# Attention and output product of a hybrid decoder block: queries' low part one slot later, transfers at other slots, second half scaled in place

## The chip, the cores and the metric

The kernel runs on one core of a Trainium2 chip. A core has a matrix engine (TensorE, "PE" in the profile; its weight loads are "PEld"), a vector engine (VectorE, "DVE"), a scalar engine (ScalarE, "ACT"), GpSimd ("POOL"), and a queue engine that here only issues transfers (SyncE, "SP"). Each engine works through its own instructions in the order in which they were written, and waits at an instruction until what it needs is there. The metric is the device time of one execution in microseconds; lower is better.

## The reference, cut to what matters

One decoder layer over 2048 tokens of width 1024, in float32. Eight attention heads with a forgetting bias run beside a gated linear recurrence; both branches are normalised and gated, joined, and multiplied by `w_out`; a residual and a gated embedding follow.

```
def forgetting_attention(q, k, v, f_logit):
    c = jnp.cumsum(jax.nn.log_sigmoid(f_logit), axis=1)
    ...
    s = einsum('bhqd,bhkd->bhqk', qi, k) * scale + (ci[..., None] - c[..., None, :])
    w = softmax(where(kpos <= qpos, s, -inf))
    return einsum('bhqk,bhkd->bhqd', w, v)
...
o_attn = forgetting_attention(q, k, v, fl)
y_attn = rmsnorm(o_attn, attn_out_gain) * silu(g_attn)
o_lru  = rg_lru(causal_depthwise_conv(x_lru, conv_w, conv_b), ...)
y_lru  = rmsnorm(o_lru, lru_out_gain) * silu(g_lru)
mix = concatenate([y_attn, y_lru]) @ w_out
h = h + rmsnorm(mix, post_gain)
h = h + sigmoid(h @ w_ple_gate + b_ple_gate) * rmsnorm(p @ w_ple, ple_gain)
```

## The kernel before, in words

Every product runs three times in a reduced float32 type: an operand is split into a high part (a rounded copy, written by ACT) and a low part (the rest, original minus high part, written by DVE or POOL), and `mm3` (L61) multiplies high by high, high by low and low by high (L66, L67, L68).

The program has four stretches: projections and recurrence (to about 1060 us), attention (to about 1647 us), the output product (to about 1945 us), and the last gate product with the output. The order of all instructions is written out by hand. In the stretches touched here it hangs on **slots**: work is put down for a slot number, and the program emits slot after slot. A slot isn't a time. It fixes only the order on each engine; a transfer on SP goes out as soon as SP comes to it and its buffer is free.

**Attention.** There are 32 stages, one for each head `h` and each group `g` of 512 queries (`stages`, L1308). Stage n takes 4g+4 slots from `t0[n]`, one slot for each block of 128 keys, so a head takes 40 slots. `run_slot` (L1436) emits for a slot, in this order: what stands in `before` (transfers above all); the score pieces of the following stage (`piece`, L1220: three products into an `sbank`, of which there are three, then one DVE instruction, L1225, that adds the bias, finds the minimum `m` and frees the bank); the product with the values of three slots ago (`add_values`, L1268); the transposes of this slot's probabilities (`turn_probs`, L1256, with their split into `th` by ACT and `tl` by DVE, L52 and L58); exponentials on ACT (L1234); and last what stands in `after`. The 4g+4 score pieces of stage n are spread over the slots of stage n-1, three slots ahead, so the short stage g=0 carries two pieces in a slot.

Around that stands other work:

- `split_u` (L1162): the queries of stage n, already loaded as `qf`, are split by `scaled_split` into `qh` (ACT, L169) and `ql` (DVE, L170), both in the `after` list of slot `lo + 1`, where the stage's scores begin at slot `s0` and `lo` lies 4 or 8 slots ahead of that.
- `load_gate` (L1301, the transfer is L1303) loads a gate tile `gs`, which has two buffers; `store_y` (L1305) stores the result from the same buffer to `ya_d`. A gate load so waits for the store of two stages ago, which stands at slot `t0[n - 1] + 6`.
- `load_piece` and `split_piece` (L1110, L1119) load the next head's keys and values in eight pieces through three `kvf` buffers, six slots ahead of their split; ACT writes the high part, POOL the low part, which frees the buffer.
- Chores (L1417 to L1427) prepare `yl2_d` (the recurrence's branch, scaled) and sums of weights: loads five slots ahead, POOL's work, stores three slots behind.

**Seam.** In the last stage (from slot `last_t0`) there are no more scores, and the first three token tiles of the output product are multiplied as `fill` (L1530) in twelve slots between the attention's own products. Their sources are loaded by `load_raw` (L1503) into `yf`, and split by `x_high` and `x_low` (L1508, L1511) into one of three operand pairs `XO`.

**Output product.** `w_out` is applied with seven products in place of eight for each half `p` of the tokens (`PRODUCTS`, L1484). A token tile of 128 rows against 512 columns is two slots of twelve matrix instructions each; tile q begins at slot `2 * (q - 3)` (`begin_of`), its high part is planned three slots ahead and its low part two. Half p works on four quarters: attention rows j=0 and j=1, recurrence rows j=2 and j=3, four tiles `t` each, which lie in sixteen tiles `X` (`load_home`, L1684) and are combined in place by DVE (L1709 to L1712, executed at L1616). The attention rows must first be scaled by the normalisation of each token; these factors are spread to rows by PE (`spread_rows`, L1566) and copied by ACT (`rows_out`). Half 0 is scaled in its home tiles. Half 1's eight tiles are, in slots 5 to 23, loaded from `ya_d` into spare tiles, scaled (`scale_rows`, L1691) and stored to `ya2_d`, and loaded from there at slots 34 to 48. Within a slot the phases LOAD, COMBINE, PREP, JOB, MUL, GATE, STORE follow one another.

Of the kernel before, what the change touches and what calls it, by code (L numbers as in the profile page):

```python
# [9 lines left out]
F32 = mybir.dt.float32  # L10
F32R = mybir.dt.float32r
# [34 lines left out]
def f32(ap):  # L46
    return ap.bitcast(F32)
# [24 lines left out]
def hymba_kernel(ctx: ExitStack, tc: tile.TileContext, x, xT, pT, w_p, w_v, w_o, w_ple, w_pg,  # L72
# [19 lines left out]
    yl2_d = dram.tile([TB, P, D], F32, name="yl2_d")  # L92
    ya2_d = dram.tile([NH, P, D], F32, name="ya2_d")
    rl_d = dram.tile([1, S], F32, name="rl_d")
# [73 lines left out]
    def scaled_split(q, hi, lo):  # L168
        nc.scalar.activation(hi, q, AF.Copy, scale=QSCALE)  # L169
        nc.vector.scalar_tensor_tensor(out=lo, in0=q, scalar=QSCALE, in1=f32(hi), op0=ALU.mult, op1=ALU.subtract)  # L170
# [990 lines left out]

    def split_u(u):  # L1162
        if u.qf is not None:
# [137 lines left out]
    def load_gate(h, g, u):  # L1301
        u.gs = av.tile([P, 512], F32, name="gs")
        nc.sync.dma_start(out=u.gs, in_=gT_d[h, :, g * 512:(g + 1) * 512])  # L1303
# [15 lines left out]
    def at(d, slot, f):  # L1319
        d.setdefault(max(slot, 0), []).append(f)  # L1320
# [22 lines left out]

    def do_split(n):
        split_u(units[n])
# [90 lines left out]
    def run_slot(t, fill=None):  # L1436
# [48 lines left out]
    tiles_ = [(i, p, t) for i, p in PRODUCTS for t in range(4)]  # L1485
    X, banks, raws = [], {}, {}

# [9 lines left out]
    def source_of(q):  # L1497
        i, p, t = tiles_[q]
        if i == 2 or (i, p) == (4, 1):
            return raws[q]  # L1500
        return X[{4: 8, 1: 0, 6: 0, 7: 4, 5: 8, 3: 12}[i] + t]

# [8 lines left out]
    def x_low(q):  # L1511
        nc.vector.tensor_tensor(out=XO[q % 3][1], in0=source_of(q), in1=f32(XO[q % 3][0]), op=ALU.subtract)
# [53 lines left out]
    def spread_rows(p):  # L1566
        for t in range(0, 8, 4):
            b = G_.b[p, t] = bank3()
            for i in range(4):
                c = 8 * p + t + i  # L1570
                nc.tensor.transpose(b[:, i * P:(i + 1) * P], rstd_a[:, c:c + 1].broadcast_to([P, P]), ident)

    def rows_out(p):
        for t in range(0, 8, 4):
            nc.scalar.activation(U2_[2 * p + t // 4], G_.b.pop((p, t)), AF.Copy)

# [4 lines left out]

    MR, U2_, U3_, XT, MT = [], [], [], [], []
    turn_ = [0]
# [10 lines left out]
    def open_left():  # L1594
        pA_stack.close()
        l4 = pool_(ctx, "l4")
        MT.extend(l4.tile([P, D], F32, name=f"mt{i}") for i in range(2))
        XT.extend(l4.tile([P, D], F32, name=f"xt{i}") for i in range(3))
        XT.insert(1, X[15])
        G_.pgain = l4.tile([P, D], F32, name="pgain")  # L1600
        G_.bgate = l4.tile([P, D], F32, name="bgate")
# [16 lines left out]
    def plan_q(q):  # L1618
        i, p, t = tiles_[q]
        s = begin_of(q)  # L1620
        if i == 2 or (i, p) == (4, 1):
            if q > 3:
                plan(s - 7, LOAD, lambda: load_raw(q))
        if q > 3:
            plan(s - 3, PREP, lambda: x_high(q))
            plan(s - 2, PREP, lambda: x_low(q))
# [54 lines left out]
    def tokens_of(p, t):  # L1681
        return ya_d[:, :, (8 * p + t) * P:(8 * p + t + 1) * P].rearrange("h p t -> p h t")

    def load_home(p, j, t):  # L1684
        o = X[4 * j + t]
        if j < 2 and p == 0:
            nc.sync.dma_start(out=o.rearrange("p (h t) -> p h t", t=P), in_=tokens_of(0, 4 * j + t))
# [3 lines left out]
    def scale_rows(o, p, n):  # L1691
        o = o.rearrange("p (h t) -> p h t", t=P)
        rho = U2_[2 * p + n // 4][:, n % 4 * P:(n % 4 + 1) * P]
        tt(o, o, rho.unsqueeze(1).broadcast_to([P, NH, P]), ALU.mult)

    for n in range(8):
        o = lambda n=n: X[13 + n % 3]
        plan(5 + 2 * n, LOAD, lambda n=n, o=o: nc.sync.dma_start(out=o().rearrange("p (h t) -> p h t", t=P),
                                                                in_=tokens_of(1, n)))
        plan(8 + 2 * n, JOB, lambda n=n, o=o: scale_rows(o(), 1, n))  # L1700
        plan(9 + 2 * n, STORE, lambda n=n, o=o: nc.sync.dma_start(out=ya2_d[n], in_=o()))
    for p, times in ((0, (7, 9, 4, 24, 15, 17, 26, 29)), (1, (34, 42, 50, 58, 53, 55, 66, 68))):
        for t in range(4):
            for j in range(4):
                plan(times[j] + (t if p == 0 and j > 1 else 2 * t), LOAD, lambda p=p, j=j, t=t: load_home(p, j, t))
            if p == 0:
                for j in range(2):
                    plan((11, 13)[j] + 2 * t, JOB, lambda j=j, t=t: scale_rows(X[4 * j + t], 0, 4 * j + t))
            plan(times[4] + 2 * t, JOB, lambda t=t: tt(X[8 + t], X[4 + t], X[8 + t], ALU.add))  # L1709
            plan(times[5] + 2 * t, JOB, lambda t=t: tt(X[4 + t], X[t], X[4 + t], ALU.subtract))  # L1710
            plan(times[6] + 2 * t, JOB, lambda t=t: tt(X[t], X[8 + t], X[t], ALU.subtract))
            plan(times[7] + 2 * t, JOB, lambda t=t: tt(X[12 + t], X[12 + t], X[t], ALU.subtract))  # L1712

# [191 lines left out]
```

## Time and profile before

| | us |
|---|---|
| three timed runs | 2148.05, 2146.4, 2148.24 |
| their median | 2148.05 |
| the profiled execution's own time | 2146.39 |
| its span, first to last instruction | 2144.6 |
| PE busy | 2092.8 (98%) |
| DVE busy | 1624.0 (76%) |
| ACT busy | 1146.0 (53%) |
| POOL busy | 734.4 (34%) |
| moved by DMA | 527.31 MB, mean 246 GB/s |

A row of a group or a wait has the source line (L1225), the engine, and the tiles as out<-in. In the view of waits a row says which instruction waited for which, the total, how often, and the longest. In the view of windows a row has the stretch, its length, the busy time of each engine with its count of instructions in brackets, then the granted PE clock (1.00 is full), the share of the DMA engines that was busy, and GB/s. In the view in order of time a row has start, length, engine, line, and in square brackets the idle time of the engine just before it with what ended it. "SPq" is SP's queue.

### The profile page before, as it was taken

What the parts mean: (1) busy time and instruction counts of PE and PEld (TensorE: products, weight loads), DVE (VectorE), ACT (ScalarE), POOL (GpSimd) and SP (SyncE); (2) the same over time, 40 slices, a digit from 0 to 9 for tenths busy, and PEclk for the clock granted to TensorE, in tenths of its full rate; (3) what the DMA queues carried; (4) which work ended last, traced back from release to release, by engine and by line L of the source; (5) the groups of instructions that cost most, each with busy time, mean ns of one, the idle gap of its engine ahead of it and who ended that gap; (6) DMA issues with size and microseconds to landing.
All of it is one profiled execution on the core that took longest, in us unless ns stands there. A gap on an engine that the chain in (4) does not pass through costs nothing.

```text
span 2144.6 us, 31680 instructions
## 1 busy us (share of the span) xinstructions
PE 2092.8 (98%) x10586; PEld 1748.6 (82%) x10586; DVE 1624.0 (76%) x2693; ACT 1146.0 (53%) x1871; POOL 734.4 (34%) x633
## 2 busy tenths in 40 slices
PE   8899999999999999999999999999999999999999
PEld 6788888888988898888878788888787878888887
DVE  7677988696858877885578788887785677876665
ACT  7435755434337766663366676767674343442222
POOL 4834455332113335632035665665543000000000
PEclk9899999999999999999999999999999999999999
DMA  8498898987888889887666776777554977665553
GB/s 319 183 325 287 296 344 299 356 308 288 286 276 272 279 257 298 272 274 248 229 194 213 234 209 205 224 232 229 167 165 156 310 269 246 231 215 168 181 173 118
DMA packets 277139, 527.31 MB, mean 246 GB/s; under 512 B 27360, under 2 KB 94192, under 8 KB 276976
## 3 DMA queue, kind: packets, MB, share of 16 engines
q1 hardware_dynamic: 276832, 525.25, 73.4%
q8 instruction: 83, 1.36, 0.3%
q14 instruction: 80, 0.66, 0.1%
q10 hardware_dynamic: 144, 0.05, 0.0%
HBM read 318.75 MB, written 206.44 MB: 245 GB/s over the span
## 4 chain that ended last, share of the span: by engine, by line
PE 77%; DMA 7%; issue 5%; POOL 5%; DVE 3%; ACT 2%; SPq 1%; POOLq 0%; DVEq 0%; ACTq 0%
PE bank L67 15%; PE bank L66 15%; PE bank L68 15%; PE pbank L68 7%; PE pbank L66 7%; PE pbank L67 7%; PE sbank L66 2%; PE tbank L1261 2%; PE sbank L68 2%; PE sbank L67 2%; DMA kvf<-kT_d 1%; DMA ya_d<-gs 1%; PE obank L67 1%; PE obank L68 1%; PE obank L66 1%
## 5 line engine op out<-in xcount | busy, mean ns | idle before, releaser
L66 PE MATMUL bank<-XH,op 128*128 128x512 f32 x876 | 347.4, 397 | 0.0
L67 PE MATMUL bank<-XL,op 128*128 128x512 f32 x876 | 346.1, 395 | 0.0
L68 PE MATMUL bank<-XH,op 128*128 128x512 f32 x876 | 345.8, 395 | 0.0
L364 DVE TENSOR_TENSOR c<-bank,c 128x512 f32<-128x512 f32 x280 | 187.0, 685 | 124.2 <-PE bank L68 117.9
L58 DVE TENSOR_TENSOR tl<-tbank,th 128x512 fp32r<-128x512 f32 (+1 forms) x320 | 191.2, 607 | 72.8 <-ACT th L52 69.6
L52 ACT ACTIVATE th<-tbank 128x512 fp32r<-128x512 f32 (+1 forms) x320 | 167.5, 529 | 116.9 <-PE tbank L1261 112.3
L68 PEld LDWEIGHTS bank<-XH,op 128*128 128x128 f32 x876 | 164.7, 188 | 39.2
L66 PEld LDWEIGHTS bank<-XH,op 128*128 128x128 f32 x876 | 164.7, 188 | 39.2 <-issue 0.5
L67 PEld LDWEIGHTS bank<-XL,op 128*128 128x128 f32 x876 | 164.8, 188 | 38.9 <-issue 0.5
L1234 ACT ACTIVATE pr<-pr,m 128x640 f32<-128x640 f32 (+7 forms) x124 | 151.9, 1225 | 51.1 <-DVE m L1225 50.1
L1261 PE MATMUL tbank<-ident,pr 128*128 128x128 f32 x1088 | 172.0, 273 | 0.0
L152 POOL TENSOR_TENSOR rsm<-rs,mhalf 128x1 f32<-128x1 f32 x16 | 8.7, 541 | 445.1 <-DVE rs L151 445.1
L1261 PEld LDWEIGHTS tbank<-ident,pr 128*128 128x128 f32 x1088 | 134.2, 140 | 28.4
L66 PE MATMUL sbank<-kh,qh 128*128 128x512 f32 (+3 forms) x320 | 137.0, 428 | 20.2 <-DVE m L1225 19.3
L66 PE MATMUL obank<-th,vh 128*128 128x512 f32 (+1 forms) x320 | 123.9, 387 | 0.8 <-ACT th L52 0.8
L286 ACT ACTIVATE op<-wf 128x512 fp32r<-128x512 f32 (+1 forms) x96 | 60.0, 630 | 113.2 <-PE bank L68 85.7
L67 PE MATMUL obank<-tl,vh 128*128 128x512 f32 (+1 forms) x320 | 118.6, 371 | 1.3 <-DVE tl L58 0.2
L68 PE MATMUL obank<-th,vl 128*128 128x512 f32 (+1 forms) x320 | 117.2, 366 | 0.0
L68 PE MATMUL sbank<-kh,ql 128*128 128x512 f32 (+3 forms) x320 | 116.4, 364 | 0.0
L67 PE MATMUL sbank<-kl,qh 128*128 128x512 f32 (+3 forms) x320 | 116.3, 364 | 0.0
L67 PE MATMUL bank<-op,XH 128*128 128x258 f32 x328 | 94.9, 289 | 6.9 <-POOL op L292 4.9
L286 ACT ACTIVATE op<-ws 128x512 fp32r<-128x512 f32 (+1 forms) x72 | 45.0, 628 | 99.5 <-PE bank L68 42.2
(305 smaller groups left out, 5849.3 us busy)
## 6 DMA issues: line engine op xcount, KB each, us to landing
wo_d<-op SPq DMA_DIRECT2D x140, 512.0 KB, 4.4
op<-wo_d SPq DMA_DIRECT2D x79, 512.0 KB, 4.8
wf<-in_w_p_dram SPq DMA_DIRECT2D x80, 256.0 KB, 4.9
wh<-wo_d SPq DMA_DIRECT2D x61, 256.0 KB, 4.1
wl<-wo_d SPq DMA_DIRECT2D x61, 256.0 KB, 4.3
vo_d<-op SPq DMA_DIRECT2D x28, 516.0 KB, 3.7
wst<-wt_d SPq DMA_DIRECT2D x56, 256.0 KB, 3.5
X<-ya_d SPq DMA_DIRECT2D x24, 512.0 KB, 5.3
```

What stands on the lines that cost most here:

```text
L52: nc.scalar.activation(hi, src, AF.Copy)
L58: eng.tensor_tensor(out=lo, in0=src, in1=f32(hi), op=ALU.subtract)
L66: nc.tensor.matmul(out, lhsT=wh, rhs=xh, start=start, stop=False)
L67: nc.tensor.matmul(out, lhsT=wh, rhs=xl, start=False, stop=False)
L68: nc.tensor.matmul(out, lhsT=wl, rhs=xh, start=False, stop=stop)
L152: nc.gpsimd.tensor_tensor(out=o, in0=t, in1=mhalf[:, :n], op=ALU.pow)
L286: nc.scalar.activation(op[:, :n], self.source(i, hf), AF.Copy)
L364: nc.vector.tensor_tensor(out=o, in0=x, in1=y, op=ALU.add)
L1234: nc.scalar.activation(pr[0][:, :L], pr[0][:, :L], AF.Exp, bias=m2, scale=-1.0, accum_out=u.r4[:, i:i + 1])
L1261: nc.tensor.transpose(b[:, i * P:(i + 1) * P], u.P[i][:, sb * P:(sb + 1) * P], ident)
```

## The change

1. `split_u` takes a part: the high part stays in slot `lo + 1`, the low part goes to `lo + 2`.
2. Transfers in attention: the gate load goes from no earlier than `t0[n - 1] + 7` to no earlier than `t0[n - 1] + 10`; the loads of key and value pieces from six to four slots ahead of their split; the stores of the chores from three to five slots behind their work.
3. Seam: token tile 0 is loaded seven slots before `last_t0` into the free `bias` buffer and split at slots +1 and +2 (before: loaded at +1, split at +4 and +5). Tiles 1 to 5 are now loaded and split within the last stage (before: 1 to 3). The fill goes from slots +7 to +18 to slots +5 to +16.
4. Output product: half 1's scaling through `ya2_d` is gone. Its tiles are loaded from `ya_d` into their homes at slots 28 to 40 and scaled there at slots 35 to 48; the homes are other tiles than before (`home`), with four of them (`A1`) in the tiles of the last stretch. Half 1's factors are spread at slot 26 (before 6). The combinations of half 1 are at slots 50, 57, 66 and 74 (before 53, 55, 66 and 68).
5. With that, the weights of the last gate product move to other tiles and its first two splits to slots 66 and 70 (before 77 and 80); the load of `bgate` moves from slot 61 to slot 104.

```
-            scaled_split(u.qf, u.qh, u.ql)
+            nc.scalar.activation(u.qh, u.qf, AF.Copy, scale=QSCALE)
+        elif u.qf is not None:
+            nc.vector.scalar_tensor_tensor(out=u.ql, in0=u.qf, scalar=QSCALE, in1=f32(u.qh),
+                                           op0=ALU.mult, op1=ALU.subtract)
...
-        at(after, min(lo + 1, s0 - 1) if n > 1 else 0, lambda n=n: do_split(n))
+        at(after, lo + 1 if n > 1 else 0, lambda n=n: split_u(units[n], 0))
+        at(after, lo + 2 if n > 1 else 0, lambda n=n: split_u(units[n], 1))
...
-        at(before, max(t0[n] - 4, t0[n - 1] + 7) if n else t0[n] + 1, lambda h=h, g=g, n=n: load_gate(h, g, units[n]))
+        at(before, max(t0[n] - 4, t0[n - 1] + 10) if n else t0[n] + 1, lambda h=h, g=g, n=n: load_gate(h, g, units[n]))
...
-            at(before, a - 6, lambda h=h, p_=p_: load_piece(h, p_))
+            at(before, a - 4, lambda h=h, p_=p_: load_piece(h, p_))
...
-    at(before, a + 3, lambda h_=h_, n=n, i=i: h_(n, i))
+    at(before, a + 5, lambda h_=h_, n=n, i=i: h_(n, i))
...
+    def load_first():
+        raws[0] = pA.tile([P, D], F32, name="yf", tag="bias", bufs=1)
+        nc.sync.dma_start(out=raws[0], in_=yl2_d[0])
+
+    at(before, last_t0 - 7, load_first)
...
-    for q, a, z in ((0, 1, 4), (1, 2, 7), (2, 4, 10), (3, 6, 14)):
+    for q, a, z in ((1, 1, 4), (2, 2, 8), (3, 4, 11), (4, 6, 15), (5, 12, 19)):
...
+    at(after, last_t0 + 1, lambda: x_high(0))
+    at(after, last_t0 + 2, lambda: x_low(0))
...
-        run_slot(t, fill if last_t0 + 7 <= t < t0[NS] + AHEAD else None)
+        run_slot(t, fill if last_t0 + 5 <= t < last_t0 + 17 else None)
...
-    for p, a in ((0, 4), (1, 6)):
+    for p, a in ((0, 4), (1, 26)):
...
+    def home(p, j, t):
+        return A1[t] if (p, j) == (1, 0) else X[4 * (j - p) + t]
...
+        if j < 2:
+            nc.sync.dma_start(out=o.rearrange("p (h t) -> p h t", t=P), in_=tokens_of(p, 4 * j + t))
         else:
-            nc.sync.dma_start(out=o, in_=ya2_d[4 * j + t] if j < 2 else yl2_d[8 * p + t + 4 * (j == 2)])
+            nc.sync.dma_start(out=o, in_=yl2_d[8 * p + t + 4 * (j == 2)])
+
+    def scale_home(p, j, t):
+        o = home(p, j, t).rearrange("p (h t) -> p h t", t=P)
+        c = (XT[3] if p else X[12])[:, (4 * j + t) * P:(4 * j + t + 1) * P]
+        tt(o, o, c.unsqueeze(1).broadcast_to([P, NH, P]), ALU.mult)
...
-    for n in range(8):
-        o = lambda n=n: X[13 + n % 3]
-        plan(5 + 2 * n, LOAD, lambda n=n, o=o: nc.sync.dma_start(out=o().rearrange("p (h t) -> p h t", t=P),
-                                                                in_=tokens_of(1, n)))
-        plan(8 + 2 * n, JOB, lambda n=n, o=o: scale_rows(o(), 1, n))
-        plan(9 + 2 * n, STORE, lambda n=n, o=o: nc.sync.dma_start(out=ya2_d[n], in_=o()))
-    for p, times in ((0, (7, 9, 4, 24, 15, 17, 26, 29)), (1, (34, 42, 50, 58, 53, 55, 66, 68))):
+    for p, times in ((0, (7, 9, 4, 24, 11, 13, 15, 17, 26, 30)), (1, (28, 34, 42, 50, 35, 42, 50, 57, 66, 74))):
...
-    for k, s in enumerate((77, 80, 84, 88, 92, 96, 99, 102)):
+    for k, s in enumerate((66, 70, 83, 87, 91, 95, 99, 102)):
...
-    plan(61, LOAD, lambda: nc.sync.dma_start(out=G_.bgate, in_=rows[2:3, :].broadcast_to([P, D])))
+    plan(104, LOAD, lambda: nc.sync.dma_start(out=G_.bgate, in_=rows[2:3, :].broadcast_to([P, D])))
```

More of the change, by code (lines that the diff above doesn't have):

```diff
@@ L92, in hymba_kernel @@
     yl2_d = dram.tile([TB, P, D], F32, name="yl2_d")
-    ya2_d = dram.tile([NH, P, D], F32, name="ya2_d")
     rl_d = dram.tile([1, S], F32, name="rl_d")
@@ L1160, in load_u, with split_u @@
             u.dg.append((L - n, dg))
-    def split_u(u):
-        if u.qf is not None:
+    def split_u(u, part):
+        if u.qf is not None and part == 0:
             u.qh = ap.tile([P, 512], F32R, name="qh", bufs=2)
             u.ql = ap.tile([P, 512], F32R, name="ql", bufs=2)
-            scaled_split(u.qf, u.qh, u.ql)
+            nc.scalar.activation(u.qh, u.qf, AF.Copy, scale=QSCALE)
+        elif u.qf is not None:
+            nc.vector.scalar_tensor_tensor(out=u.ql, in0=u.qf, scalar=QSCALE, in1=f32(u.qh),
+                                           op0=ALU.mult, op1=ALU.subtract)
     def mask_u(u):
@@ L1342, in do_load @@
         load_u(*stages[n], units[n])
-    def do_split(n):
-        split_u(units[n])
     for n in range(1, NS):
@@ L1472, in run_slot @@
             f()
+    raws = {}
+    def load_first():
+        raws[0] = pA.tile([P, D], F32, name="yf", tag="bias", bufs=1)
+        nc.sync.dma_start(out=raws[0], in_=yl2_d[0])
+    at(before, last_t0 - 7, load_first)
     for t in range(last_t0 + 1):
@@ L1485, in hymba_kernel @@
     tiles_ = [(i, p, t) for i, p in PRODUCTS for t in range(4)]
-    X, banks, raws = [], {}, {}
+    X, banks = [], {}
     def bank3():
@@ L1500, in source_of @@
             return raws[q]
-        return X[{4: 8, 1: 0, 6: 0, 7: 4, 5: 8, 3: 12}[i] + t]
+        return home(p, {4: 2, 1: 0, 6: 0, 7: 1, 5: 2, 3: 3}[i], t)
     def load_raw(q):
@@ L1571, in spread_rows, with rho @@
                 nc.tensor.transpose(b[:, i * P:(i + 1) * P], rstd_a[:, c:c + 1].broadcast_to([P, P]), ident)
+    def rho(p, n):
+        return (XT[3] if p else X[12])[:, n * P:(n + 4) * P]
     def rows_out(p):
         for t in range(0, 8, 4):
-            nc.scalar.activation(U2_[2 * p + t // 4], G_.b.pop((p, t)), AF.Copy)
+            nc.scalar.activation(rho(p, t), G_.b.pop((p, t)), AF.Copy)
     G_.b = {}
@@ L1580, in hymba_kernel @@
         plan(a + 1, COMBINE, lambda p=p: sums_root(p))
-    MR, U2_, U3_, XT, MT = [], [], [], [], []
+    MR, U2_, U3_, XT, MT, A1 = [], [], [], [], [], []
     turn_ = [0]
@@ L1598, in open_left @@
         XT.extend(l4.tile([P, D], F32, name=f"xt{i}") for i in range(3))
-        XT.insert(1, X[15])
+        XT.insert(1, X[11])
+        A1.extend((MT[0], MT[1], XT[0], XT[2]))
         G_.pgain = l4.tile([P, D], F32, name="pgain")
@@ L1621, in plan_q @@
         if i == 2 or (i, p) == (4, 1):
-            if q > 3:
+            if q > 5:
                 plan(s - 7, LOAD, lambda: load_raw(q))
-        if q > 3:
+        if q > 5:
             plan(s - 3, PREP, lambda: x_high(q))
@@ L1682, in tokens_of @@
         return ya_d[:, :, (8 * p + t) * P:(8 * p + t + 1) * P].rearrange("h p t -> p h t")
+    def home(p, j, t):
+        return A1[t] if (p, j) == (1, 0) else X[4 * (j - p) + t]
     def load_home(p, j, t):
-        o = X[4 * j + t]
-        if j < 2 and p == 0:
-            nc.sync.dma_start(out=o.rearrange("p (h t) -> p h t", t=P), in_=tokens_of(0, 4 * j + t))
-        else:
-            nc.sync.dma_start(out=o, in_=ya2_d[4 * j + t] if j < 2 else yl2_d[8 * p + t + 4 * (j == 2)])
[L1691 to L1694, printed above, removed]
@@ L1696, in hymba_kernel @@
[L1696 to L1702 removed]
+        o = home(p, j, t)
@@ L1703, in hymba_kernel @@
         for t in range(4):
+            a11, a21, a22, a12 = (lambda p=p, j=j, t=t: home(p, j, t) for j in range(4))
             for j in range(4):
                 plan(times[j] + (t if p == 0 and j > 1 else 2 * t), LOAD, lambda p=p, j=j, t=t: load_home(p, j, t))
[L1706 to L1709, printed above, removed]
@@ L1710, in hymba_kernel @@
-            plan(times[5] + 2 * t, JOB, lambda t=t: tt(X[4 + t], X[t], X[4 + t], ALU.subtract))
-            plan(times[6] + 2 * t, JOB, lambda t=t: tt(X[t], X[8 + t], X[t], ALU.subtract))
-            plan(times[7] + 2 * t, JOB, lambda t=t: tt(X[12 + t], X[12 + t], X[t], ALU.subtract))
+            for j in range(2):
+                plan(times[4 + j] + 2 * t, JOB, lambda p=p, j=j, t=t: scale_home(p, j, t))
+            for n, (o, x_, y_, op) in enumerate(((a22, a21, a22, ALU.add), (a21, a11, a21, ALU.subtract),
+                                                 (a11, a22, a11, ALU.subtract), (a12, a12, a11, ALU.subtract))):
+                plan(times[6 + n] + 2 * t, JOB, lambda o=o, x_=x_, y_=y_, op=op: tt(o(), x_(), y_(), op))
@@ L1727, in gate_load @@
     def gate_load(k):
-        stage[k] = XT[2 + k % 2]
+        stage[k] = (XT[3], G_.bgate)[k % 2]
         nc.sync.dma_start(out=stage[k], in_=w_pg[:, k])
     def gate_high(k):
-        wG[k] = ([G_.r3.tile([P, D], F32R, name=f"wg{n}", tag=f"X{n}", bufs=1) for n in (2 * k, 2 * k + 1)] if k < 6 else
+        wG[k] = ([G_.r3.tile([P, D], F32R, name=f"wg{n}", tag=f"X{n}", bufs=1)
+                  for n in ((12, 13), (14, 15), (0, 1), (2, 3), (4, 5), (6, 7))[k]] if k < 6 else
                  WO[0][2 * k - 12:2 * k - 10])
@@ L1795, in load_e @@
         def load_e():
-            u.et = X[13 + n % 2]
+            u.et = X[9 + n % 2]
             nc.sync.dma_start(out=u.et, in_=e_d[ts, :])
```

2 lines of the change are left out of this document (1 added, 1 removed).

## The prediction, made before the change was run

> **What bounds the kernel now.** I read the page first, then the windows of attention and output, then who waited for whom, then single waits in order of time.
>
> ```profile
> span 2144.6 us, 31680 instructions
> PE 2092.8 (98%) x10586; PEld 1748.6 (82%) x10586; DVE 1624.0 (76%) x2693; ACT 1146.0 (53%) x1871; POOL 734.4 (34%) x633
> ```
>
> PE is busy for 98% of the span, and the change takes no matrix instruction away. So it can win only what PE loses in waits, and what the clock loses behind them. The view of waits, for PE from 1060 us to the end:
>
> ```profile
> PE sbank L66 <- DVE m L1225: 19.3, 19, 3.1
> PE pbank L68 <- DVE xl L1512: 3.5, 2, 3.2
> PE tbank L1557 <- DVE sa L1561: 2.4, 1, 2.4
> PE bank L68 <- DVE xl L1512: 1.6, 1, 1.6
> PE obank L66 <- ACT th L52: 0.8, 1, 0.8
> ```
>
> Attention loses 19.3 us, always to DVE, which frees the score bank. The output product loses 3.5 us, the seam 2.4 and 1.6. The windows show what follows the three longest waits:
>
> ```profile
> core 0: us, PE busy (x) PEld busy (x) DVE busy (x) ACT busy (x) POOL busy (x), PEclk, DMA share, GB/s
> 1500.00:1520.00 20.00, 16.89 (x90) 14.44 (x89) 14.64 (x38) 9.67 (x17) 11.12 (x13) 0.91 0.68 221
> 1646.00:1664.00 18.00, 15.60 (x74) 12.94 (x73) 10.82 (x16) 6.18 (x9) 4.58 (x2) 0.91 0.84 285
> 1664.00:1708.00 44.00, 44.00 (x202) 36.57 (x201) 26.21 (x25) 14.64 (x22) 0.00 (x0) 1.00 0.98 304
> 1708.00:1736.00 28.00, 24.55 (x95) 19.38 (x95) 21.23 (x21) 10.55 (x15) 0.00 (x0) 0.88 0.94 332
> 1736.00:1945.00 209.00, 209.00 (x926) 173.15 (x925) 159.91 (x197) 90.31 (x127) 0.55 (x1) 1.00 0.68 223
> ```
>
> The granted clock falls below 1.00 in exactly these. A clock of 0.91 over 20 us costs 20 x 0.09 = 1.8 us, over 18 us 1.6 us, and 0.88 over 28 us 3.4 us: 6.8 us together. From 1736 us PE never idles: nothing can be won there, only lost.
>
> **Part 1: the queries' low part (attention).** Who made DVE late? Its own waits from 1074 to 1605 us:
>
> ```profile
> DVE tl L58 <- ACT th L52: 50.4, 78, 1.5
> DVE ql L170 <- ACT qh L169: 24.0, 23, 3.1
> ```
>
> and one of them in order of time, first DVE, then PE:
>
> ```profile
> 1217.76 0.69 DVE L170 SCALAR_TENSOR_TENSOR ql<-qf,qh 128x512 fp32r<-128x512 f32 x1 [1.28 <-ACT qh L169]
> 1218.37 0.68 DVE L1225 CUSTOM_DVE_ANT_0 pr<-sbank,bias 128x512 f32<-128x512 f32 x1
> 1219.12 0.50 PE L66 MATMUL sbank<-kh,qh 128*128 128x512 f32 x1 [1.35 <-DVE m L1225]
> ```
>
> DVE idles 1.28 us at `ql`, because ACT came to `qh` only then; the next score piece is taken 1.28 us late, and PE, out of banks, waits 1.35 us. The longest case:
>
> ```profile
> 1502.60 0.63 ACT L169 ACTIVATE qh<-qf 128x512 fp32r<-128x512 f32 x1 [2.54 <-DMA qf<-qT_d]
> 1503.26 0.69 DVE L170 SCALAR_TENSOR_TENSOR ql<-qf,qh 128x512 fp32r<-128x512 f32 x1 [3.06 <-ACT qh L169]
> 1504.62 0.50 PE L66 MATMUL sbank<-kh,qh 128*128 128x512 f32 x1 [3.11 <-DVE m L1225]
> ```
>
> A slot later the high part is long written and this idle time is gone. The 0.69 us of work stays: it moves behind the next slot's `tl`. Nothing is late for it, since the scores begin at `s0`, two slots or more after `lo + 2`. Before 1080 us lie waits that have no `ql` ahead of them:
>
> ```profile
> PE sbank L66 <- DVE m L1225: 2.1, 2, 1.6
> ```
>
> so 19.3 - 2.1 = 17.2 us in 17 waits are open to the change. In the two cases shown, idle time is 4.34 of 4.46 us of PE's wait, 97%: 16.7 us. What I keep back is the moved `ql`: in a stage of four slots DVE is nearly full, and 0.69 us there may leave a rest, taken as 0.17 us for each of the 16 common waits, 2.7 us. That gives 14.0 us. Bounds: only the longest wait goes (3.1), or all 17.2. With the longest wait goes its clock loss, 1.8. PE also restarts slowly: after the 1504.62 wait the first product takes 0.50 us; the group's mean without waits is 0.395 to 0.397, so about 0.1 a wait, 17 x 0.1 = 1.7.
>
> ```profile
> L67 PE MATMUL bank<-XL,op 128*128 128x512 f32 x876 | 346.1, 395 | 0.0
> ```
>
> **Part 2: transfers in attention.** The view of waits for SP's queue from 1080 to 1605 us, and ACT's for keys from 1074 us on,
>
> ```profile
> SPq L1303 <- DMA ya_d<-gs: 128.1, 30, 8.2
> SPq L1116 <- POOL kl L58: 49.6, 13, 8.2
> SPq L1398 <- POOL kvs L1395: 17.8, 7, 7.0
> ACT kh L52 <- DMA kvf<-kT_d: 8.0, 6, 2.2
> ```
>
> and the next head's `ql` of the same stage as the one at 1217.76:
>
> ```profile
> 1286.77 0.69 DVE L170 SCALAR_TENSOR_TENSOR ql<-qf,qh 128x512 fp32r<-128x512 f32 x1 [1.28 <-ACT qh L169]
> ```
>
> SP stands still for 128.1 us at gate loads, 4.3 us at each, and everything behind them (`qf`, biases, masks, key pieces) goes out late. Four slots instead of one behind the store are about 7 us (a head's 40 slots take 1286.77 - 1217.76 = 69 us, so 1.7 a slot); most of the wait should go, and most of the 49.6. SP is on nobody's path but through `qf` (the 1502.60 row) and `kvf`. The former is in part 1 already. I count zero for the rest; bounds: the 8.0 us that ACT waits for keys won in full, or two slots a head lost (a rival below).
>
> **Part 3: the seam.** The 2.4 us wait:
>
> ```profile
> 1653.06 1.06 ACT L1509 ACTIVATE xh<-yf 128x1024 fp32r<-128x1024 f32 x1 [5.88 <-DMA yf<-yl_d]
> 1654.15 1.23 DVE L1512 TENSOR_TENSOR xl<-yf,xh 128x1024 fp32r<-128x1024 f32 x1 [4.34 <-ACT xh L1509]
> 1655.30 1.28 DVE L1561 TENSOR_REDUCE sa<-tbank 128x4 f32<-128x512 f32 x2
> ```
>
> Token tile 4 came late from DMA, and the sums behind it on DVE held up PE's transposes. Tiles 4 and 5 now load at +6 and +12, under the fill, so 2.4 + 1.6 (clock) = 4.0 us go. The fill's own wait is another matter:
>
> ```profile
> 1614.07 1.66 DVE L1289 TENSOR_TENSOR gs<-on,gs 128x512 f32<-128x512 f32 x1
> 1618.51 1.22 DVE L1512 TENSOR_TENSOR xl<-yf,xh 128x1024 fp32r<-128x1024 f32 x1
> 1619.78 0.50 PE L68 MATMUL bank<-wa,xl 128*128 128x512 f32 x1 [1.61 <-DVE xl L1512]
> ```
>
> Tile 0's low part comes three slots sooner, but the fill starts two sooner, and `xl` now stands right behind that 1.66 us `gs`: done at 1614.07 + 1.66 + 1.22 = 1617. PE now arrives at 1619.78 - 1.61 = 1618.2; two slots of value products and transposes sooner, without a fill in them, are some 2 us: 1616. So a wait of about the same size: I count zero, with bounds +1.6 and -1.5. Slots +17 and +18 lose the fill as cover; one fill and two value products still stand between the last transpose and its product, and what they don't cover is a part of one `th` and one short `tl`, under 1 us.
>
> **Part 4: the output product.** A slot is 12 x 209/926 = 2.71 us. DVE's work there, by groups from 1664 to 1720 us, then the stall, and the page's row of the loads of attention rows (5.3 us to landing):
>
> ```profile
> L1616 DVE TENSOR_TENSOR X<-X,u 128x1024 f32<-128x1024 f32 x15 | 18.0, 1219 | 0.0
> L1512 DVE TENSOR_TENSOR xl<-yf,xh 128x1024 fp32r<-128x1024 f32 x4 | 4.9, 1221 | 4.1 <-ACT xh L1509 4.1
> L1193 DVE TENSOR_TENSOR wa<-wst,wa 128x512 fp32r<-128x512 f32 x7 | 4.8, 692 | 7.2 <-ACT wa L1189 7.2
> 1718.76 0.79 PE L68 MATMUL pbank<-wb,xl 128*128 128x512 f32 x1 [3.16 <-DVE xl L1512]
> X<-ya_d SPq DMA_DIRECT2D x24, 512.0 KB, 5.3
> ```
>
> By the plan, slots 15 to 22 hold four `xl`, six weight parts, twelve half-0 scalings and combinations, and four half-1 scalings: 4 x 1.22 + 6 x 0.69 + 16 x 1.22 = 28.5 us for 8 x 2.71 = 21.7. DVE falls 6.8 us behind; `xl` is planned 5.4 ahead and takes 1.2, so it covers 4.2, and 2.6 would be the wait: measured 3.2. Without the four half-1 scalings it falls behind by 2.0, at most 2.4 on the way: covered. So 3.5 + 3.4 (clock) = 6.9 us go; bounds 0 and 6.9. DMA loses eight stores and their reloads, 16 x 512 KB, and was at 0.98 here. The scalings come back at slots 35 to 48, where the fullest pair of slots (34 to 37) holds one `xl`, two weight parts, one eviction (of a weight part's size) and two of 1.22: 5.7 us against 5.4. That is at most 1.3 behind, with 4.2 of cover: zero. Half 1's strided loads have seven slots, 19 us, for their 5.3. The later transposes of its factors are the same work. Zero too; if the cover were gone, a stall of the size above.
>
> **A rule weighed.** The Trainium skill, "TensorE: Matmul & The Clock Gate", "Why this matters for your kernels", puts the loss of clock at PE gaps of some 3 us and more. By it the wait of 2.4 us would cost no clock, and the sum would be 1.6 less; the row of 1646 to 1664 us has 0.91 all the same, and the sum goes by the row.
>
> **The sum.** 14.0 + 1.8 + 1.7 + 4.0 + 6.9 = 28.4 us, against the profiled execution's own 2146.39 (span 2144.6 and 1.8 around it): 2118.0. The runs' median is 1.7 above that execution; I leave the forecast at 2118.
>
> **The rivals.**
>
> 1. *DVE is the bound, not its idle time* (0.18). The wait follows `ql` into the next slot. For: 0.69 us in a stage already tight. Against: the 97% above. Then of the 17.2 only 3.1 and about a quarter of the rest go, 6.6, with 1.8 of clock: 6.6 + 1.8 + 4.0 + 6.9 = 19.3 less, 2127.
> 2. *The output stall comes back elsewhere* (0.12), in the fullest slots or at a strided load that is late: 28.4 - 6.9 = 21.5 less, 2125.
> 3. *The other side: key pieces come too late* (0.07). Load 6 of a head now lands when ACT needs it or up to 2.2 us after (the ACT row). If SP isn't freed, two slots less are 3.4 us more of ACT blocked with `th` behind it, and PE follows; past about 2.4 us of PE's wait the clock goes too, 1.7 a time. 7 heads x (3.4 + 1.7) = 36 us against 28.4: 2154, slower. Against: SP's 128 and 50 us are what makes it late today. It decides once the piece lands over two slots late.
> 4. *The change doesn't do what it says* (0.05): DVE waits as long for ACT at the next instruction, the seam and output waits reappear one step on. 2146.
>
> **How the numbers follow.** Forecast 0.58, its own range 2109 to 2123. No change is within 0.2%, some 4.3 us, about what a measurement of this kernel can tell. Faster: the forecast and rivals 1 and 2, 0.88; same: rival 4, 0.05; slower: rival 3, 0.07. Low end: all waits, clock and restart, 17.2 + 1.8 + 1.7 + 4.0 + 1.6 + 6.9 = 33.2, gives 2113; with a good half of the 8.0 that ACT waits for keys 2108. The high end takes in rivals 1 and 2 with a few us for a new small wait: 2132.
>
> **What would show it.** Right: `ql` with no idle time before it; PE's wait for `m` down to some 5 us; SP's wait at gate loads down to a fifth; clock 1.00 after 1500, 1650 and 1710 us; PE unbroken from 1664 us on. Wrong: PE waits of old size one slot after `ql`'s old place (rival 1); a PE wait for `xl` between 1735 and 1945 us (rival 2); ACT's wait for `kvf` well over 8 us (rival 3).

## The result, and the profile after

The changed kernel takes 2119.48 us (median of 4 runs, 2117.58 to 2120.41), the kernel before 2148.14 us on the same chip (4 runs, 2146.4 to 2151.26): a ratio of 0.9864, 95% interval 0.9847 to 0.9881. Forecast were 2118.0 us and a range of 2108 to 2132. The sum was nearly right. Three of its four parts were mis-sized, in directions that partly cancelled, and the fourth had the right size for the wrong reason.

The profiled execution took 2120.41 us. Its page:

```profile
span 2118.6 us, 31621 instructions
PE 2084.5 (98%) x10586; PEld 1744.3 (82%) x10586; DVE 1619.9 (76%) x2693; ACT 1144.9 (54%) x1871; POOL 736.2 (35%) x633
```

PE executes the same 10586 instructions and is busy 8.3 us less. Some 5 us of that are the clock: by the windows of the prediction and those below, losses of 1.8, 1.6 and 3.4 us are gone and one of 1.7 is new. The two largest rows of PE's waits from 1060 us to the end (engine, tile, line, who was waited for, then us in total, times, longest):

```profile
PE bank L68 <- DVE xl L1519: 3.4, 1, 3.4
PE sbank L66 <- DVE m L1227: 2.7, 4, 1.6
```

Of attention's 19.3 us for `m` 2.7 are left. The waits for `pbank` (3.5) and `tbank` (2.4) are gone. The fill's wait for `xl` has grown from 1.6 to 3.4 us. The windows, columns as in the prediction:

```profile
1500.00:1520.00 20.00, 20.00 (x118) 17.24 (x117) 17.60 (x47) 14.84 (x23) 10.50 (x12) 1.00 0.57 166
1600.00:1608.00 8.00, 7.14 (x28) 5.81 (x29) 3.87 (x6) 1.27 (x3) 2.98 (x2) 0.79 0.56 185
...
1646.00:1664.00 18.00, 18.00 (x81) 14.89 (x80) 5.45 (x5) 6.21 (x9) 0.00 (x0) 1.00 0.96 296
...
1708.00:1736.00 28.00, 28.00 (x125) 23.16 (x125) 22.63 (x27) 11.53 (x18) 0.00 (x0) 1.00 0.73 217
1736.00:1945.00 209.00, 209.00 (x933) 173.01 (x932) 160.68 (x199) 87.78 (x122) 1.64 (x3) 1.00 0.65 210
```

The granted clock is 1.00 where it had been 0.91, 0.91 and 0.88, and a new low place, 0.79, stands behind the fill's wait: 8 x 0.21 = 1.7 us.

How much each stage gave can be read from four matrix products that both kernels execute: the first transpose of probabilities behind the score pieces, the last score product, the first product of the output stage, and the last one. In the timeline of before:

```profile
1082.12 0.38 PE L1261 MATMUL tbank<-ident,pr 128*128 128x128 f32 x2
...
1603.84 0.39 PE L68 MATMUL sbank<-kh,ql 128*128 128x512 f32 x1
...
1664.37 0.48 PE L66 MATMUL pbank<-wa,xh 128*128 128x512 f32 x1
...
2139.63 0.28 PE L68 MATMUL pbank<-wa,h 128*128 128x256 f32 x1
```

and in that of after:

```profile
1082.68 0.49 PE L1263 MATMUL tbank<-ident,pr 128*128 128x128 f32 x3
...
1585.86 0.39 PE L68 MATMUL sbank<-kh,ql 128*128 128x512 f32 x1
...
1645.13 0.48 PE L66 MATMUL pbank<-wa,xh 128*128 128x512 f32 x1
...
2113.64 0.28 PE L68 MATMUL pbank<-wa,h 128*128 128x256 f32 x1
```

| stage, start to start | before | after | difference | forecast |
|---|---|---|---|---|
| attention | 521.72 | 503.18 | -18.5 | -17.5 (parts 1 and 2) |
| seam | 60.53 | 59.27 | -1.3 | -4.0 |
| output product | 475.26 | 468.51 | -6.75 | -6.9 |

With 0.56 us lost before the first mark that is the 26.0 us between the two spans. The medians differ by 28.7; of the two profiled executions, before's was the fastest of its four runs and after's the slowest (in a second profile of the same kernel, `after_again` below, attention is 20.0 us shorter than before, and the other two stages differ as in the table). Such stage differences are given for the experiments too, always against before's profile.

In attention, the waits of SP's queue from 1080 to 1605 us and those of ACT from 1074 us on:

```profile
SPq L1305 <- DMA ya_d<-gs: 46.0, 17, 5.0
SPq L1115 <- POOL kl L58: 33.9, 14, 3.6
```

```profile
ACT vh L52 <- DMA kvf<-v_d: 2.3, 1, 2.3
```

SP's wait at gate loads fell from 128.1 to 46.0 us, that at key pieces from 49.6 to 33.9. Other waits of SP grew: all its rows together fell only from some 308 to 280 us. So SP stands still nearly as long as before, but at other places. ACT's 8.0 us at key pieces are gone; one wait of 2.3 us at a piece of the values is left. VectorE's idle time at `ql`, 24.0 us before, has no row any more.

### The profile page after: what moved, and what is told of

The parts are those of the page before. It is cut to its first block, busy times and chain, and to the rows that moved or that the text cites. A ratio compares the mean times of both kernels' runs of the same rounds, so it can differ in the third digit from the quotient of the medians.

```text
span 2118.6 us, 31621 instructions
## 1 busy us (share of the span) xinstructions
PE 2084.5 (98%) x10586; PEld 1744.3 (82%) x10586; DVE 1619.9 (76%) x2693; ACT 1144.9 (54%) x1871; POOL 736.2 (35%) x633
## 4 chain that ended last, share of the span: by engine, by line
PE 84%; POOL 4%; DMA 4%; DVE 3%; issue 3%; ACT 1%; SPq 0%; DVEq 0%; POOLq 0%; ACTq 0%
PE bank L66 15%; PE bank L67 15%; PE bank L68 15%; PE pbank L68 7%; PE pbank L66 7%; PE pbank L67 7%; PE tbank L1263 3%; PE sbank L66 3%; PE sbank L68 2%; PE sbank L67 2%; PE obank L67 2%; PE obank L68 2%; PE obank L66 2%; POOL s L690 1%; DMA dg<-nb_d 1%
```

## The experiments

### Attention: which part gave the 18.5 us

**The low part back in its old slot.**

```
-        at(after, lo + 2 if n > 1 else 0, lambda n=n: split_u(units[n], 1))
+        at(after, lo + 1 if n > 1 else 0, lambda n=n: split_u(units[n], 1))
```

> The changed kernel with one thing undone: the queries' low part goes back to the slot of the high part; transfers, seam and output stay changed. Theory A (DVE stood idle at the low part until ACT had written the high part, and PE ran out of score banks behind it): DVE's wait at ql comes back at 15 to 24 us in some 20 times, PE's wait for m goes from 2.7 to 14 to 19 us, the time from 2119.5 to 2133 to 2138. Theory B (SP, freed from its waits, was what helped; the slot of the low part is a side matter): PE's wait for m stays under 6 us, the time under 2123. Theory C (DVE is simply full there): PE's wait for m the same in both, some 3 us, time 2119 to 2121.

Measured: 2131.97 us (4 runs, 2130.56 to 2134.76), ratio to before 0.9926 (0.9912 to 0.9941): 12.5 over the changed kernel. VectorE's and PE's waits:

```profile
DVE ql L1167 <- ACT qh L1165: 19.5, 21, 1.7
```

```profile
PE sbank L66 <- DVE m L1227: 12.7, 18, 1.6
```

The idle time at `ql` and the many waits for `m` are back, so the mechanism is the forecast one. But attention still is 7.9 us shorter than before, so the low part did not bring all of it: 7.9 us is what the transfers' new slots bring with `ql` in its old place. The long wait of before, 3.1 us behind the late `qf`, did not come back (the longest is 1.6), and neither did the loss of clock behind it:

```profile
1495.00:1515.00 20.00, 19.79 (x115) 16.70 (x114) 18.69 (x49) 13.37 (x23) 10.68 (x12) 1.00 0.79 223
```

**The low part alone**, the kernel before with only this step of the change (and `split_u` in its two parts):

```
-        at(after, min(lo + 1, s0 - 1) if n > 1 else 0, lambda n=n: do_split(n))
+        at(after, lo + 1 if n > 1 else 0, lambda n=n: split_u(units[n], 0))
+        at(after, lo + 2 if n > 1 else 0, lambda n=n: split_u(units[n], 1))
```

> The kernel before with one thing changed: the low part a slot behind the high part. Theory A: PE's wait for m falls from 19.3 to 3 to 6 us and the half clock behind 1504 us goes, 15 to 18 us less than before, 2130 to 2133. Theory B (the transfers' new slots are needed): no more than 5 us less, 2143 or more, with PE still waiting 14 us or more for m.

Measured: 2135.75 us (4 runs, 2130.95 to 2138.05), 0.994 (0.9924 to 0.9956): 12.4 under before, less than Theory A's 15 to 18. It is the same figure as from the other side, but the runs spread over 7 us, so the agreement to 0.1 us is chance. The profiled execution is the fastest of them; in it attention is 11.8 us shorter than before. What PE and ACT wait for there:

```profile
PE sbank L66 <- DVE m L1228: 8.6, 7, 2.1
...
PE sbank L68 <- DVE ql L1168: 2.0, 5, 0.7
```

```profile
ACT kh L52 <- DMA kvf<-kT_d: 13.5, 6, 3.8
ACT vh L52 <- DMA kvf<-v_d: 1.7, 2, 1.3
```

With `ql` out of the way, 8.6 us of waits for `m` remain, longer and fewer, and ACT's wait for pieces of keys and values has grown from 8.0 to 15.2 us. `th`, the probabilities' high part, stands behind those pieces on ACT, and VectorE waits for `th` 69.1 us where it was 50.4. The next limit was the transfers, which the forecast had put at zero.

**The transfers back** (the low part stays a slot later):

```
-        at(before, max(t0[n] - 4, t0[n - 1] + 10) if n else t0[n] + 1, ...load_gate...)
+        at(before, max(t0[n] - 4, t0[n - 1] + 7) if n else t0[n] + 1, ...load_gate...)
...
-            at(before, a - 4, lambda h=h, p_=p_: load_piece(h, p_))
+            at(before, a - 6, lambda h=h, p_=p_: load_piece(h, p_))
...
-        at(before, a + 5, lambda h_=h_, n=n, i=i: h_(n, i))
+        at(before, a + 3, lambda h_=h_, n=n, i=i: h_(n, i))
```

> The changed kernel with the gate loads, the loads of key pieces and the chores' stores back at their old slots. Theory A: SP's wait at gate loads goes from 46 back to about 128 us, but PE's wait for m stays under 6 us and the time within 3 us of 2119.5, since SP is on the path only through a late qf, and DVE no longer waits for that at once. Theory B: PE's waits in attention come back by 8 us or more, time 2127 or more.

Measured: 2129.32 us (4 runs, 2128.47 to 2129.98), 0.9912 (0.9897 to 0.9927): 9.8 over the changed kernel, where Theory A had at most 3. PE's waits for `m` and `ql` are 8.6 us, against 2.9 in the changed kernel. ACT's waits for transfers, from 1074 us on:

```profile
ACT kh L52 <- DMA kvf<-kT_d: 12.7, 7, 3.1
ACT qh L1165 <- DMA qf<-qT_d: 1.1, 2, 0.9
```

So the transfers are worth some 10 us once the low part has moved, and 7.9 us before that. Each step put in alone, by the marks, 11.8 and 7.9 us add up to 19.7, inside the stage's whole gain of 18.5 to 20.0. Each taken out, by the medians, 12.5 and 9.8 add up to 2 to 4 us more than that gain, no more than executions of one kernel differ. The two steps nearly add up.

**Only the key pieces back at six slots ahead, and only the gate loads back**, one at a time:

> The changed kernel with only the loads of key and value pieces back at six slots ahead. New theory D (undoing all transfers cost 9.8 us, against the forecast's zero, because ACT then waits 1.4 to 3.2 us a head for the sixth key load, which goes out behind SP's wait for a buffer and five bias and mask loads; with four slots ahead these go out before that wait): ACT's wait for kh comes back at 8 to 14 us in some 6 times, and 6 to 10 us of time come back, 2126 to 2130. Rival E (the gate loads, whose wait on SP fell from 134 to 46 us, did it): within 3 us of 2119.5.

> The changed kernel with only the gate loads back at seven slots. Theory D: SP's wait at gate loads rises to 110 us or more, ACT's wait for kh stays under 3 us, and the time within 3 us of 2119.5. Rival E: 2126 or more.

Measured: the pieces 2134.9 us (4 runs, 2133.3 to 2137.56), 0.9937 (0.9921 to 0.9954), 15.4 over the changed kernel, far more than expected and more than all three transfers together; the gate 2126.59 us (4 runs, 2125.69 to 2129.88), 0.99 (0.9884 to 0.9917), 7.1 over, where Theory D had at most 3. So neither of the two theories holds alone: both loads matter. With the pieces back, SP's and ACT's waits are

```profile
SPq L1115 <- POOL kl L58: 55.3, 8, 8.8
```

```profile
ACT kh L52 <- DMA kvf<-kT_d: 18.8, 7, 3.7
ACT qh L1165 <- DMA qf<-qT_d: 5.2, 6, 1.3
```

and with the gate back ACT waits for the values' pieces:

```profile
ACT vh L52 <- DMA kvf<-v_d: 9.8, 5, 2.9
```

A piece that is asked for two slots sooner does not come sooner. Its buffer isn't free until POOL has written the low part of the piece three before it; SP stands at that load, up to 8.8 us, and behind it in SP's order stand bias and mask rows and the next pieces. In one head SP stands from 1329.4 to 1337.8 us; then the bias, four mask rows and the key piece that ACT will wait for go out one behind the other. Asked for later, the load finds its buffer free or nearly so (3.6 us at most), and the others have gone out meanwhile.

The moves do not add up: 15.4 and 7.1 against 9.8 for all three. Why the pieces alone cost more than all three stays open. The rows show where the time goes: ACT waits 24.0 us instead of 13.8 (12.7, and 1.1 for `qf`), PE waits 13.4 us for `m` and `ql` instead of 8.6, and the clock falls to 0.91 in this stretch and in that from 1420 to 1440 us, while with all three back it is 1.00 from 1085 to 1595 us:

```profile
1355.00:1375.00 20.00, 18.35 (x104) 16.02 (x103) 17.35 (x44) 13.13 (x24) 10.29 (x13) 0.91 0.68 231
```

The third move, the chores' stores, was not tried alone.

### Seam: the fill's wait

**The first low part of the tokens one slot sooner.** In the changed kernel's seam VectorE, POOL and PE do this:

```profile
1596.82 1.78 DVE L1291 TENSOR_TENSOR gs<-on,gs 128x512 f32<-128x512 f32 x1
1598.52 2.28 DVE L1519 TENSOR_TENSOR xl<-yf,xh 128x1024 fp32r<-128x1024 f32 x1
```

```profile
1596.77 1.27 POOL L1195 TENSOR_TENSOR wb<-wst,wb 128x512 fp32r<-128x512 f32 x1 [1.63 <-ACT wb L1191]
1598.26 1.46 POOL L1195 TENSOR_TENSOR wb<-wst,wb 128x512 fp32r<-128x512 f32 x1 [0.22 <-ACT wb L1191]
1599.68 2.03 POOL L1300 TENSOR_TENSOR on<-on 128x512 f32<-128x512 f32 x1
```

```profile
1600.86 0.67 PE L68 MATMUL bank<-wa,xl 128*128 128x512 f32 x1 [3.44 <-DVE xl L1519]
```

`gs` takes 1.78 us where its fastest take 0.68, and `xl` 2.28 instead of 1.22, both while POOL works. A slot sooner `xl` stands ahead of `gs`:

```
-    at(after, last_t0 + 2, lambda: x_low(0))
+    at(after, last_t0 + 1, lambda: x_low(0))
```

> The changed kernel with token tile 0's low part in slot +1 of the last stage instead of +2, ahead of the attention's last scaling and gating on DVE. Theory F (the fill's wait of 3.4 us stems from the order on DVE: the low part stands behind gs, and both run slow beside POOL): the wait falls under 1 us and the half clock behind it goes, 3 to 5 us less than the changed kernel, 2115 to 2117. Rival (DVE then waits for ACT's high part and the attention's own tl is late): the wait only moves, 2119 or more.

Measured: 2115.23 us (4 runs, 2113.2 to 2116.46), 0.9844 (0.9828 to 0.9859). On another chip, beside the changed kernel itself:

> The changed kernel with the first low part of the tokens made one slot sooner, a second time, to compare it on one chip with the changed kernel itself. Theory F (the fill's wait and the half clock behind it cost 3 to 5 us): 2113.5 to 2117, 3 to 6 us under the changed kernel in this call. Rival (the 4.2 us seen between runs of two chips were those chips): within 1.5 us of it.

> The changed kernel once more, unaltered, on the same chip as the two runs before and the one behind: 2117.5 to 2121.5, and a fill's wait of about 3 us for xl in its profile, if that wait belongs to the kernel and not to the one profiled execution.

Measured: 2113.86 us (5 runs, 2111.92 to 2115.47), 0.9841 (0.9825 to 0.9858), against the changed kernel's 2119.01 (4 runs, 2118.21 to 2123.28), 0.9868 (0.985 to 0.9886). It is 5.15 us faster, and no run of the one reaches into the runs of the other; it beats both kernels. By the marks the seam is 6.6 us shorter than before's in both its profiles, against 1.3 in both of the changed kernel's. PE has no wait between 1590 and 1950 us, and the clock and `xl` in its second profile are:

```profile
1585.00:1610.00 25.00, 24.04 (x135) 19.95 (x134) 12.85 (x20) 16.37 (x28) 12.51 (x9) 1.00 0.56 181
```

```profile
1592.55 1.23 DVE L1519 TENSOR_TENSOR xl<-yf,xh 128x1024 fp32r<-128x1024 f32 x1 [0.74 <-ACT xh L1516]
```

The gain is the 3.44 us of the wait and the 1.7 us of clock behind it.

**The fill two slots later**, at +7 to +18 in place of +5 to +16:

```
-        run_slot(t, fill if last_t0 + 5 <= t < last_t0 + 17 else None)
+        run_slot(t, fill if last_t0 + 7 <= t < last_t0 + 19 else None)
```

> The changed kernel with the fill back at slots +7 to +18, tile 0 still loaded and split early. Theory F: the fill now starts some 2.3 us later, so its wait falls to about 1 us and the clock stays full, 2 to 5 us less than the changed kernel, 2115 to 2118; the slots left without fill cost nothing either way. Rival (the earlier fill is what won the seam): 2121 or more.

Measured: 2118.5 us (4 runs, 2118.14 to 2120.42), 0.9862 (0.9844 to 0.988): no difference. PE's waits from 1590 us on:

```profile
PE obank L67 <- DVE tl L58: 3.3, 2, 3.1
```

The 2 to 5 us that were expected did not come. The fill no longer waits, but `tl` stands behind the same `gs` and `xl` on VectorE, and PE waits for that instead. What had to move was the low part, not its user. Nor did the rival's loss come: the fill's two slots were worth nothing either way.

### Output product: what made the stall

**The output part alone**: the kernel before with half 1's rows loaded into their homes and scaled there, as in the change, and nothing else of it.

> The kernel before with only the output product changed: half 1 loaded into its homes and scaled there, with what goes with it; attention and seam as before. Theory A: the two waits of PE for xl near 1710 and 1719 us (3.5 us) and the half clock behind them go, 5 to 7 us less than before, 2141 to 2143, with PE unbroken from 1664 to 1945 us. Rival: the stall comes back in slots 30 to 48 or at a late load, 0 to 3 us less, 2145 or more.

Measured: 2142.7 us (10 runs, 2139.56 to 2146.22), 0.9976 (0.9966 to 0.9985), 5.4 under before; by the marks the output stage is 6.75 us shorter, to 0.01 us the same as in the changed kernel. The stall is gone; this doesn't tell why, since the change takes away both VectorE's scalings and the transfers around them. Two runs put back one of these each.

**Eight unused adds on VectorE** in the slots of the old scalings:

```
+    for n in range(8):
+        plan(8 + 2 * n, JOB, lambda n=n: tt(X[13 + n % 3], X[8 + n % 4], X[8 + n % 4], ALU.add))
```

> The changed kernel with eight unused 128x1024 adds put on VectorE in the first slots of the output product (one every second slot), into tiles that nothing reads; no transfer is added, and nothing of the result is left out. Theory G (the backlog of VectorE is what made the stall in the output product, as the forecast worked it out): each add takes about 1.2 us, so by the eighth slot-pair VectorE is again 6 to 8 us behind, PE's wait for xl near 1690 to 1710 comes back with 2 to 4 us and the half clock behind it, and the time is 4 to 7 us over the changed kernel: 2123 to 2127. Rival H (the stall came from the loads and stores of the other half's rows, which the change also took away): VectorE has room here, PE has no wait in 1664 to 1945, and the time stays within 2 us: 2118 to 2121.5.

**Eight unused loads and stores of half 1's rows** in the slots of the old ones, without a scaling:

```
+    for n in range(8):
+        plan(5 + 2 * n, LOAD, lambda n=n: nc.sync.dma_start(out=X[13 + n % 3]..., in_=tokens_of(1, n)))
+        plan(9 + 2 * n, STORE, lambda n=n: nc.sync.dma_start(out=ya2_d[n], in_=X[13 + n % 3]))
```

> The changed kernel with the traffic that the change took away put back without its scaling: eight loads of half 1's rows into tiles that nothing reads, and eight stores of them to a scratch tensor, in the first slots of the output product; nothing of the result is left out. Theory G (VectorE's backlog made the stall): PE has no wait in 1664 to 1945, 2118 to 2121.5. Rival H (the loads and stores made it, through SP's order or the DMA engines, by making weights or rows late): PE waits again 2 to 4 us with the half clock behind, 2123 to 2127.

Measured, beside 2119.01 of the changed kernel on the same chip: with the adds 2119.64 us (4 runs, 2118.5 to 2120.76), 0.9867 (0.985 to 0.9883); with the transfers 2124.69 (4 runs, 2122.67 to 2129.59), 0.9894 (0.9874 to 0.9913), 5.7 more. By the marks the output stage takes 468.51 us with the adds, as in the changed kernel, and 474.47 with the transfers, which brings back 6.0 of the 6.75. The same 54.5 us of output products, from the first one on, in before, with the adds and with the transfers:

```profile
1664.30:1718.80 54.50, 51.05 (x230) 41.69 (x228) 35.17 (x34) 17.53 (x27) 0.00 (x0) 0.99 0.97 309
```

```profile
1643.20:1697.70 54.50, 54.50 (x243) 45.15 (x242) 41.07 (x40) 20.04 (x30) 0.00 (x0) 1.00 0.78 245
```

```profile
1643.30:1697.80 54.50, 51.73 (x226) 42.45 (x225) 29.29 (x29) 18.18 (x27) 0.00 (x0) 0.98 1.03 324
```

With the adds VectorE works 41.07 us there, 5.9 more than in before, and PE never waits. It even works 26 us without a break:

```profile
1676.00:1702.00 26.00, 26.00 (x116) 21.56 (x115) 26.00 (x27) 9.82 (x14) 0.00 (x0) 1.00 0.52 174
```

With the transfers it works only 29.29, and PE waits as before did:

```profile
PE pbank L68 <- DVE xl L1520: 2.8, 1, 2.8
```

So VectorE's amount of work wasn't the cause; the forecast's reading falls. SP's queue and ACT in before, 1675 to 1726 us, and with the transfers, 1655 to 1706 us:

```profile
SPq L1698 <- DMA ya_d<-X: 18.2, 5, 4.7
```

```profile
ACT wa L1189 <- DMA wst<-in_w_o_dram: 21.5, 5, 6.7
```

```profile
SPq L1725 <- DMA ya_d<-X: 12.8, 5, 4.2
```

```profile
ACT wa L1192 <- DMA wst<-in_w_o_dram: 20.5, 6, 5.8
```

Half 1's loads go through three spare tiles, and each waits for the store out of such a tile to land. SP stands at it for up to 4.7 us, five times; behind it in its order stand the loads of `w_out`. ACT gets the weights late, VectorE has the weights' low part in its order ahead of `xl`, and PE waits for `xl`. In the changed kernel and with the adds, ACT has no wait for weights in those 51 us.

The order on SP isn't the only way in which the transfers can make weights late. In before, the chain of work that ended last holds, shortly ahead of PE's wait at 1718.76, two loads of weights (start and length):

```profile
1695.52 6.04 DMA wst<-in_w_o_dram
1706.84 5.89 DMA wst<-in_w_o_dram
```

The median time of such a load from issue to landing is the last figure here, over the 51 us named above, in before and in the changed kernel:

```profile
wst<-in_w_o_dram SPq DMA_DIRECT2D x8, 256.0 KB, 5.6
wst<-in_w_o_dram SPq DMA_DIRECT2D x7, 256.0 KB, 4.3
```

It is 5.6 with the added transfers too, and 4.3 with the adds, while the DMA engines' share is 0.97 and 1.03 against 0.78. So a load that has gone out also lands 1.3 us later. That the transfers made the stall is shown; how much of it went through SP's order and how much through busier DMA engines, these runs don't separate.

## Why the prediction was right, and where it was wrong

**Part 1, mis-sized.** "14.0 us" of waits, 1.8 of clock and 1.7 of restarts, 17.5 in all: the low part measured 12.5 taken out and 12.4 put in alone. The mechanism holds (the idle time at `ql` goes and comes with the waits for `m`), and to keep back 2.7 us was the right kind of term. What it kept back was too little: the wait went on to the next late thing, ACT's key pieces, 8.6 us of waits in 7 places. The longest wait and its clock, 3.1 and 1.8 us, were counted here, but `undo_split` has neither, with the low part in its old slot: the transfers alone bring `qf` in time. "Nothing is late for it" wasn't quite so either: PE waits 2.0 us for `ql` where the pieces are still early, 0.2 in the changed kernel.

**Part 2, wrong.** "I count zero for the rest" was the failed step. The transfers brought 7.9 us with `ql` in its old slot, and 9.8 with it moved. The bound of 8.0, ACT's wait for keys won in full, was about the right size, and zero was taken in its place without a reason: the prediction itself names `kvf` as a way on which SP is on a path. The row of SP's 128.1 and 49.6 us showed the cause. With `ql` gone, ACT's wait at the pieces grew to 15.2 us, but the worth of the transfers grew by only some 2 us, which is no more than executions differ. That parts 1 and 2 together came out at 18.5 against 17.5 is luck: two errors that cancel.

**Part 3, wrong.** The 2.4 us wait and its clock went, as forecast, and tiles 4 and 5 come in time. The fill's own wait, "I count zero, with bounds +1.6 and -1.5", became 3.44 us from 1.61, and 1.7 us of clock came with it, 3.5 together. The forecast had `xl` done 1.0 us behind PE's arrival. PE arrived 0.60 us after `gs` began (1600.86 - 3.44 - 1596.82), not 1.93 (1616 - 1614.07), which is 1.3 more; and `xl` took 2.28 us, not 1.22, which is 1.1 more: 1.0 + 1.3 + 1.1 = 3.4. By this 0.5 us of the forecast 4.0 would be left; 1.3 were measured. `low_1` shows that this one order was worth 5 us.

**Part 4, right in size, wrong in cause.** 6.9 forecast, 6.75 measured. But "DVE falls 6.8 us behind" isn't what made the stall: eight adds more did nothing, eight transfers brought it back. The agreement of 2.6 computed with 3.2 measured was an accident. The prediction's own rows spoke against a backlog: VectorE worked 26.21 of the 44 us ahead of the stall, and its 7.2 us of idle time at `wa` stand there as waits for ACT. The transfers, whose sixteen moves and DMA share of 0.98 it noted, got no price. The zeros behind it held: PE has no wait from 1736 to 1945 us, and half 1's loads and scalings at their new places cost nothing.

**The rule weighed.** The Trainium skill, "TensorE: Matmul & The Clock Gate", "Why this matters for your kernels", puts the loss of the clock at gaps of some 3 us and more. The runs bear out neither it nor a shorter limit. `rows_alone`, around a wait of 2.8 us at the seam, and `undo_split`, around the fill's wait of 3.45 us:

```profile
1654.00:1662.00 8.00, 6.09 (x22) 4.96 (x23) 7.91 (x12) 4.26 (x6) 4.58 (x2) 0.79 0.92 327
```

```profile
1611.00:1619.00 8.00, 6.41 (x32) 5.32 (x33) 5.25 (x6) 1.90 (x4) 4.05 (x4) 1.00 0.68 215
```

The shorter wait lost 1.7 us of clock, the longer none; the fill's wait of 3.44 us in the changed kernel lost 1.7. The same page, "What's actually happening", describes a window of 3413 ns that runs on its own; that a wait's place in such a window decides would fit, and no run here tests it.

**The rivals.** Rival 3, key pieces too late, had its place right and its sign wrong: asking sooner, not later, makes them late. Rival 1 (the wait follows `ql`) happened in small, 2.0 to 3.6 us, in the three experiments that leave the pieces early. Rivals 2 and 4 did not happen. Of what was to be seen, `ql` without idle time, the clock after 1500, 1650 and 1710 us and PE unbroken from 1664 us on came true; PE's wait for `m` is 2.7, not "some 5", and SP's wait at gate loads fell to 36%, not "a fifth".

## What to carry to other kernels

A wait of a queue engine that only issues transfers gets onto the path when something urgent stands behind the waiting load in its order; here that was worth 8 to 10 us of attention. So read who is queued behind it, not whose data it carries, and ask for a transfer no sooner than its buffer can be free: two slots sooner cost 15.4 us here. A term that comes out in the right size is not thereby shown: put back the work and the transfers separately, since both left together. And where a row gives a bound for a wait, do not put zero in its place without a reason: the bound of 8.0 us was close to what the transfers brought.

## What the runs showed of the hardware that was not expected

**VectorE beside POOL.** In these traces, instructions of VectorE that read two tensors from SBUF take up to 2.6 times as long while POOL works. The queries' low part by form, in before and in after (durations in ns: least, median, most):

```profile
L170 DVE SCALAR_TENSOR_TENSOR ql<-qf,qh x30: 691/752/1785, 1080.0 to 1572.7; 128x512 fp32r<-128x512 f32 x30
```

```profile
L1167 DVE SCALAR_TENSOR_TENSOR ql<-qf,qh x30: 658/719/1443, 1082.4 to 1556.9; 128x512 fp32r<-128x512 f32 x30
```

Sorted by whether a POOL instruction ran at the same time: in before, the 5 `ql` with POOL idle took 691 to 694 ns, the 7 wholly beside POOL 1648 to 1785; `gs` 681 to 691 against 689 to 1789. `tl`, which reads one of its two tensors from PSUM, shows nothing of it: of those of 128x512, 51 with POOL idle took 677 to 694 ns, 100 wholly beside it 673 to 693. It doesn't strike each time: in after, 14 `ql` wholly beside POOL took 681 to 1443 ns, and in `low_1_again` a `gs` and an `xl` beside POOL took 0.69 and 1.24 us. The Trainium skill, "GPSIMD Engine Reference", "8. Key points", says that POOL shares its SBUF interfaces with VectorE, and names VectorE instructions with two SBUF inputs among those that contend with it; the sizes are this case's. The forecast had 0.69 us for the moved `ql` and 1.22 for `xl`, from the undisturbed rows.
